# Recurrence products on the full 128x128 array with one readout burst per pair, a pinned first solve, and LoRA grouped with the first block as 336 and 384 columns

## The chip, the core and the metric

The kernel runs on one core of one Trainium2 chip. A core has five engines that run side by side, each from its own queue in order: TensorE (PE) multiplies, with a weight loader beside it (PEld); VectorE (DVE), ScalarE (ACT) and GpSimd (POOL) do elementwise work; SyncE (SP) issues most of the DMA transfers. They wait for one another through semaphores. TensorE takes two operands from the on-chip memory SBUF, a stationary one and a moving one of up to 512 columns here, and writes to PSUM.

The metric is the device time in microseconds (us), the median of three runs. Before the change it is 1944.83 us (1944.59 to 1945.52).

## The reference, cut to what matters

All arrays are float32; 256 frames (tokens), model width 4096. One layer is computed:

```python
proj = x @ w_in                       # 256 x 4096 by 4096 x 16592
fq, fk, fv, ff, r, k, v, wd, ad, z = split(proj)   # 2048 each; ff 16; wd, ad 96; z 4096
# first head group: forgetting attention, 16 heads of 128
log_f = log_sigmoid(ff + f_bias);  c = cumsum(log_f)
fox = softmax(fq.fk/sqrt(128) + c[t] - c[s], s <= t) @ fv
# second head group: RWKV-7, 32 heads of 64, after a two-tap token shift of r, k, v, wd, ad
decay = exp(-exp(-softplus(-(w0 + tanh(wd) @ w_up)) - 0.5));  a = sigmoid(a0 + ad @ a_up)
kk = normalise(k * k_k);  k = k * (1 + (a - 1) * k_a)
for t in frames:                      # state S is 64 x 64 for each head
    S = S * decay[t] + (S @ -kk[t]) (kk[t] * a[t])^T + v[t] k[t]^T
    y[t] = S @ r[t]
rwkv = groupnorm(y) * gain + bias + sum(r * k * r_k) * v
h = concat(fox, rwkv) * silu(z)
out = layernorm(2 ** 0.25 * x + h @ w_out)
```

By work this is two large products, 256 x 4096 by 4096 x 16592 and 256 x 4096 by 4096 x 4096, with attention and a recurrence of 256 steps between them.

## The kernel before, in words

**The weight products.** Every fp32 operand of a large product is cut in two fp32r numbers, hi and lo, by `split`: ACT copies the high part (L137), DVE subtracts it (L138). `mm` then makes three products for each weight tile, x_hi by w_hi, x_lo by w_hi and x_hi by w_lo (L143, L144, L145), each with a 128x128 stationary slice of x and 512 moving columns of weights. Tiles `w_5h` and `w_5l` are the parts of one weight load, and `acc` is the PSUM sum.

**The LoRA stage (L107 to L166)** comes first, while x itself arrives, in 17 pieces of one or two k-tiles. Each piece loads x, the 208 columns of wd, ad and ff (`w_lora`) and 512 columns of the first weight block, splits them, and multiplies the 208 columns into `accl0`, `accl1` and the 512 into `acc0_0_0`, `acc0_0_1`.

**The blocks.** The rest of w_in is a stream of 8 x 4 blocks: for each of eight head pairs n, block 0 holds r and k, block 1 the two v, blocks 2 and 3 attention's q and k and the gate. A block has 16 loads of 1024 columns by 128 rows (two k-tiles; SP issues them at L213), 12 products each. The load buffers form a ring of four, the hi parts of four, the lo parts of three. A name such as w0_3_7l is pair 0, block 3, load 7, low part.

**The side work.** All else runs in the gaps of the block loop: after every second (k-tile, half) step, `slot()` moves each of a list of generators one `yield` on. `ahead()` runs `lora()` and then `prepare(i)` for the 16 slices of two heads; `chain()` runs `forget()` (the forget gate, which ends with the DMA `ncd`, L346) and then `rwkv(n)` for the eight pairs; `unload` and `fox` carry q, k and the gate to the attention. `yield from wait(k)` lets k slots go by. So the slot counts set where a side product stands among the weight products. A scheduler then orders each engine's queue from the program and its own model of durations; where `tc.keep_in_program_order` is put round an instruction, it stays behind its predecessor in the program.

**`rwkv(n)` (L510 to L704)** works on one pair n: two slices u of 128 rows, each with two heads j of 64, and four chunks c of 64 frames. In order:

- `gp`: score products of each chunk, masked into `gb` and `Nb`.
- the solve (L582 to L590): 31 steps, each a DVE multiply into `prod` (L584) and a reduction into `xc` (L587), which invert the triangular matrices inside the chunks. A step works on one column more than the step before it, and `next(other)` lets the transposes of `turns()` go between. Only the first step is kept in program order. For n = 0 the attention scores `lg` (L723) and the splits of the next weights share that queue.
- the result `td` is stored and reloaded in another layout (T, X): X is the inverse, block-diagonal over the two heads.
- the chunk loop (L652 to L684): `residual(c)` makes `rh` = lt . SV (L631), copied by DVE to R; `up` = X . R (L658), copied by ACT to UV; `sp` = BKt . UV (L667), from which DVE makes the next chunk's state in SV; and `yp`, the readout (L683), eight products for each slice and chunk pair, 64 by 64 by 64.

In `rh`, `sp` and `yp` each head j has its own tile, `lt[j]`, `SV[j]`, `UV[j]`, and is zero outside its part. An operand `lt0_n` has the rows of both heads; j picks the 64 columns in which the result is wanted:

```python
nc.tensor.matmul(rh[HALF[j], u * C : (u + 1) * C], lt[j][:, u, c, 0:C], SV[j][:, u, c, :], start=True, stop=True)
```

So a product uses 128 rows and 64 stationary columns, and two of them lie side by side in the array. `up` uses a 128x128 stationary operand with 64 moving columns.

After the eight pairs the output product takes 8 x 16 loads of w_out, then the residual, LayerNorm and the store follow.

Of the kernel before, what the change touches and what calls it, by code (L numbers as in the profile page):

```python
# [10 lines left out]
F32 = mybir.dt.float32  # L11
# [49 lines left out]
QS = 2 * S // B  # L61

# [20 lines left out]
def layer(ctx: ExitStack, tc: tile.TileContext, xt, xtok, w_lora, w_main, muv, w_o, up, par, mulora, fbias, lng, lnb, cst, out):  # L83
# [27 lines left out]
    for n, (k0, k1) in enumerate(pieces):  # L111
# [3 lines left out]
        raw = spool.tile([P, 2 * LW], F32, tag="lr", name=f"lr{n}", bufs=4)  # L115
        (nc.scalar if n < 3 else nc.sync).dma_start(out=raw[:, : (k1 - k0) * LW], in_=w_lora[:, k0:k1, :].rearrange("p k c -> p (k c)"))
        l_raw.append(raw)
        raw = wpool.tile([P, 1024], F32, tag="wr", name=f"wr{n}", bufs=4)
        nc.sync.dma_start(out=raw[:, : (k1 - k0) * OB], in_=w_main[0, 0][:, k0:k1, :].rearrange("p k c -> p (k c)"))
# [34 lines left out]
    for n, (k0, k1) in enumerate(pieces):  # L154
# [303 lines left out]

    def prepare(i):
# [7 lines left out]
        if u == 0:  # L467
# [3 lines left out]
                lt=[rp.tile([P, 2, NCH, P], F32, tag=f"lt{j}", name=f"lt{j}_{n}") for j in range(2)],  # L471
# [12 lines left out]
        lt = [q["lt"][j][:, u] for j in range(2)]  # L484
        nc.scalar.copy(q["lc"][:, u, :], eL[:, :, C])
        nc.vector.scalar_tensor_tensor(lt[0][:, :, 0:C], ch(kr), nkk[:, i : i + 1], eL[:, :, 0:C], ALU.mult, ALU.mult)
        nc.vector.tensor_tensor(lt[0][:, :, C:P], ch(r), eL[:, :, 1:], ALU.mult)
# [22 lines left out]
    def rwkv(n):  # L510
# [4 lines left out]
        lc, BK, lt, bon = q["lc"], q["BK"], q["lt"], q["bon"]  # L515
        yield from wait(W["gp"])
        gp = [[pst(f"gp{n}_{u}_{j}") for j in range(2)] for u in range(2)]
        for u in range(2):
            for c in range(NCH):
                for j in range(2):  # L520
                    h = HALF[j]
                    nc.tensor.matmul(gp[u][j][:, c * P : (c + 1) * P], BK[h, u, c, :], lt[j][h, u, c, :], start=True, stop=True)  # L522
# [21 lines left out]
        for u in range(2):  # L544
            for j in range(2):
                o = HALF[1 - j]
                nc.vector.tensor_tensor(lt[j][o, u], gv[u][j][o], m(o), ALU.mult)
        SV = [rp.tile([P, 2, NCH, C], F32, tag=f"SV{j}", name=f"SV{j}_{n}") for j in range(2)]
# [537 lines left out]
```

## Time and profile before

| | |
|---|---|
| median of three runs | 1944.83 us (1944.59, 1944.83, 1945.52) |
| the profiled execution | 1945.32 us |
| its span (first to last instruction) | 1943.5 us |
| mean granted TensorE clock | 0.998 |
| PE busy | 1925.2 us, 99% |
| DVE, ACT, POOL busy | 1348.8, 962.8, 129.9 us |
| DMA traffic | 420.07 MB, 216 GB/s |
| LoRA stage on PE | from 4.24 to 70.8 us |

In the page and in the answers of the trace, busy times and starts are in us of the span's clock. A row of the timeline gives the start, the duration of one instruction in the pipeline, engine, line, operation, output tile <- input tiles, their sizes, and a count where like neighbours are put together. Matmuls overlap: what one costs is the distance from its start to that of the next, not its duration. An fp32 product (not fp32r) runs as two passes, so a product of the source counts twice there. A bracket at the end of a row says how long the engine was idle ahead of it, and what it was waiting for. The granted clock (PEclk) is the share of full speed that TensorE was given.

### The profile page before, as it was taken

How to read it: one execution, taken by the hardware profiler on the slowest of the kernel's cores; microseconds unless marked ns; L12 is line 12 of the kernel's file. 1: busy time of each engine (PE TensorE's matmuls, PEld its weight loads, DVE VectorE, ACT ScalarE, POOL GpSimd, SP SyncE). 2: the span in 40 equal slices, each digit the busy share in tenths (PEclk: the TensorE clock that was granted, in tenths of full speed). 3: DMA queues.
4: the chain of work that ended last, by engine and by line, in shares of the span. 5: the costliest groups of instructions: out<-in, count | busy, mean ns of one | idle time of the engine just before them, and what ended most of it. 6: DMA issues, size and time to landing. Idle time of an engine off the chain costs nothing.

```text
span 1943.5 us, 28242 instructions
## 1 busy us (share of the span) xinstructions
PE 1925.2 (99%) x10121; PEld 1578.9 (81%) x10121; DVE 1348.8 (69%) x2291; ACT 962.8 (50%) x1445; POOL 129.9 (7%) x207
## 2 busy tenths in 40 slices
PE   9998999999999999999999999999999999999998
PEld 8877788878887888788878887888788878888886
DVE  6577667866786678667856785778577856755555
ACT  6453465455545554465456445644564454433332
POOL 0020002000200020002000200020001000000000
PEclk9999999999999999999999999999999999999999
DMA  9577677867786768677867686778677878766664
GB/s 339 138 242 199 202 195 214 229 199 206 222 229 192 227 201 240 189 221 209 238 185 228 207 239 183 228 208 240 178 232 219 241 273 263 236 198 199 188 205 163
DMA packets 269393, 420.07 MB, mean 216 GB/s; under 512 B 142338, under 2 KB 171028, under 8 KB 269252
## 3 DMA queue, kind: packets, MB, share of 16 engines
q1 hardware_dynamic: 268820, 417.84, 72.3%
q8 instruction: 79, 1.29, 0.3%
q10 hardware_dynamic: 432, 0.43, 0.1%
q14 instruction: 62, 0.51, 0.1%
HBM read 388.55 MB, written 29.64 MB: 215 GB/s over the span
## 4 chain that ended last, share of the span: by engine, by line
PE 96%; DVE 2%; DMA 0%; issue 0%; ACT 0%; SPq 0%; ACTq 0%; DVEq 0%
PE acc L143 24%; PE acc L145 23%; PE acc L144 23%; PE oacc L853 6%; PE oacc L855 6%; PE oacc L854 6%; PE yp L683 1%; PE gp L522 1%; PE up L658 1%; PE rh L631 1%; PE sp L667 0%; DVE prod L584 0%; DVE xc L587 0%; PE tp L555 0%; PE fsp L718 0%
## 5 line engine op out<-in xcount | busy, mean ns | idle before, releaser
L587 DVE TENSOR_REDUCE xc<-prod 128x8 f32<-128x16 f32 (+30 forms) x248 | 73.1, 295 | 6.7
L584 DVE TENSOR_TENSOR prod<-Nb,xc 128x8 f32<-128x8 f32 (+30 forms) x248 | 71.4, 288 | 6.6
L138 DVE TENSOR_TENSOR w_6l<-w,w_6h 128x1024 fp32r<-128x1024 f32 x31 | 37.9, 1223 | 45.3 <-ACT w_6h L137 29.1
L714 POOL TENSOR_SCALAR_AFFINE_SELECT nb<-nb 128x128 f32<-128x128 f32 x32 | 14.5, 455 | 727.5 <-DMA nb<-ncd 284.0
L138 DVE TENSOR_TENSOR w_5l<-w,w_5h 128x1024 fp32r<-128x1024 f32 x31 | 40.5, 1308 | 32.3 <-PE acc L145 31.3
L138 DVE TENSOR_TENSOR w_8l<-w,w_8h 128x1024 fp32r<-128x1024 f32 x31 | 37.8, 1218 | 30.2 <-ACT UV L661 13.6
L137 ACT CAST w_7h<-w 128x1024 fp32r<-128x1024 f32 x31 | 32.5, 1049 | 52.1 <-DMA w<-in_w_main_dram 34.3
L138 DVE TENSOR_TENSOR w_12l<-w,w_12h 128x1024 fp32r<-128x1024 f32 x31 | 37.9, 1223 | 26.7 <-issue 12.4
L145 PE MATMUL acc<-w_7l,x 128*128 128x512 f32 x124 | 48.7, 402 | 5.4 <-DVE w_7l L138 5.4
L137 ACT CAST w_13h<-w 128x1024 fp32r<-128x1024 f32 x31 | 32.6, 1051 | 40.7 <-DMA w<-in_w_main_dram 15.3
L138 DVE TENSOR_TENSOR w_7l<-w,w_7h 128x1024 fp32r<-128x1024 f32 x31 | 37.8, 1220 | 21.5 <-ACT sl L679 8.5
L143 PE MATMUL acc<-w_7h,x 128*128 128x512 f32 x124 | 51.3, 413 | 0.0
L137 ACT CAST w_5h<-w 128x1024 fp32r<-128x1024 f32 x31 | 32.6, 1052 | 37.5 <-PE acc L144 37.5
L138 DVE TENSOR_TENSOR w_14l<-w,w_14h 128x1024 fp32r<-128x1024 f32 x31 | 37.9, 1221 | 19.0 <-issue 16.2
L137 ACT CAST w_15h<-w 128x1024 fp32r<-128x1024 f32 x31 | 32.7, 1054 | 36.9 <-PE acc L144 27.2
L143 PE MATMUL acc<-w_5h,x 128*128 128x512 f32 x124 | 50.5, 407 | 0.0
L143 PE MATMUL acc<-w_3h,x 128*128 128x512 f32 x124 | 50.2, 405 | 0.0
L138 DVE TENSOR_TENSOR w_11l<-w,w_11h 128x1024 fp32r<-128x1024 f32 x31 | 37.9, 1222 | 17.6 <-PE acc L145 16.2
L143 PE MATMUL acc<-w_8h,x 128*128 128x512 f32 x124 | 50.1, 404 | 0.1
L143 PE MATMUL acc<-w_6h,x 128*128 128x512 f32 x124 | 49.9, 402 | 0.0
L137 ACT CAST w_10h<-w 128x1024 fp32r<-128x1024 f32 x31 | 32.5, 1049 | 35.0 <-PE acc L144 30.9
L143 PE MATMUL acc<-w_2h,x 128*128 128x512 f32 x124 | 49.6, 400 | 0.0
(810 smaller groups left out, 6520.0 us busy)
## 6 DMA issues: line engine op xcount, KB each, us to landing
w<-in_w_main_dram SPq DMA_DIRECT2D x496, 512.0 KB
wo<-in_w_o_dram SPq DMA_DIRECT2D x128, 512.0 KB
bt<-bk SPq DMA_DIRECT2D x88, 128.0 KB
Nb<-nd SPq DMA_DIRECT2D x16, 512.0 KB
wr<-in_w_main_dram SPq DMA_DIRECT2D x15, 512.0 KB
hd<-hl SPq DMA_DIRECT2D x29, 256.0 KB
h<-hd SPq DMA_DIRECT2D x29, 256.0 KB
raw<-bt SPq DMA_DIRECT2D x16, 256.0 KB
```

The lines of the kernel that those rows point to most:

```text
L137: nc.scalar.copy(hi[:, :n], src[:, :n])
L138: nc.vector.tensor_tensor(lo[:, :n], src[:, :n], hi[:, :n].bitcast(F32), ALU.subtract)
L143: nc.tensor.matmul(acc[:, :n], xs[k][:, 0, tt], hi[:, o : o + n], start=(k == 0), stop=False)
L144: nc.tensor.matmul(acc[:, :n], xs[k][:, 1, tt], hi[:, o : o + n], start=False, stop=False)
L145: nc.tensor.matmul(acc[:, :n], xs[k][:, 0, tt], lo[:, o : o + n], start=False, stop=(k == KT - 1))
L522: nc.tensor.matmul(gp[u][j][:, c * P : (c + 1) * P], BK[h, u, c, :], lt[j][h, u, c, :], start=True, stop=True)
L584: first = nc.vector.tensor_tensor(prod[:, :, :, s + 1 :], nb[:, :, s : s + 1, s + 1 :].to_broadcast([P, 2, NJ, w]), xc[:, :, :, s + 1 :], ...
L587: nc.vector.tensor_reduce(xc[:, :, :, s : s + 1], prod[:, :, :, s:], AX.X, ALU.add)
L631: nc.tensor.matmul(rh[HALF[j], u * C : (u + 1) * C], lt[j][:, u, c, 0:C], SV[j][:, u, c, :], start=True, stop=True)
L853: nc.tensor.matmul(acc, ht[k][:, 0, tt], hi, start=(k == 0), stop=False)
L854: nc.tensor.matmul(acc, ht[k][:, 1, tt], hi, start=False, stop=False)
L855: nc.tensor.matmul(acc, ht[k][:, 0, tt], lo, start=False, stop=(k == KT - 1))
```

## The change

Four things are changed.

- **Full products.** `lt[0]` and `lt[1]`, `SV[0]` and `SV[1]`, and the two UV become one tile each (`LT`, `SVt`, `UVt`), with j as an inner index. `rh` and `sp` are now one product for each slice u, 128 rows by 128 stationary columns by 128 moving columns, where four products of 64 by 64 stood for a pair of slices. Only the two blocks on the diagonal are wanted, which `diagonal` picks; the other two quarters of the result are not read. R and UV are now copied one half by ACT and one half by DVE; before, DVE copied R whole and ACT both halves of UV.
- **One readout burst.** `yp` leaves the chunk loop. Its 32 products of the four chunks come in one piece behind the last `up`, and a `wait(2)` after `sp` takes the slots.
- **First solve.** For n = 0 every step's multiply stands in program order, for the other pairs the first alone, as before.
- **Columns.** The first 128 columns of the first block move to the LoRA products: 336 and 384 columns for 208 and 512. The sums are copied to `bk0_0` from both, and `lw` takes another buffer (that of `vs`).

```diff
@@ the LoRA stage
-        hi, lo = split(l_raw[n], (k1 - k0) * LW, f"wl{n}", spool, str(n % 3), 2 * LW)
+        hi, lo = split(l_raw[n], (k1 - k0) * LA, f"wl{n}", spool, str(n % 3), 2 * LA)
         for j, m in steps(k1 - k0, False):
-            mm(acc_l[m], m, k0 + j, hi, lo, j * LW, LW)
-        hi, lo = split(w_raw[n], (k1 - k0) * OB, f"wr{n}")
+            mm(acc_l[m], m, k0 + j, hi, lo, j * LA, LA)
+        hi, lo = split(w_raw[n], (k1 - k0) * LB, f"wr{n}")
         for j, m in steps(k1 - k0, k1 == KT):
-            mm(acc_0[m], m, k0 + j, hi, lo, j * OB, OB)
+            mm(acc_0[m], m, k0 + j, hi, lo, j * LB, LB)
...
-    lw = rp.tile([P, 2, LW], F32, tag="bk", name="lw")
+    lw = rp.tile([P, 2, LW], F32, tag="vs", name="lw", bufs=1)
+    bk_0 = rp.tile([P, 2, OB], F32, tag="bk", name="bk0_0")
     for m in range(2):
         nc.scalar.copy(lw[:, m, :], acc_l[m][:, :LW])
+        nc.scalar.copy(bk_0[:, m, :P], acc_l[m][:, LW:LA])
...
+    def left(t, j):
+        return t.rearrange("p u c (x j t) -> p u c j x t", x=2, j=2)[:, :, :, j]
...
@@ rwkv(n)
-        SV = [rp.tile([P, 2, NCH, C], F32, tag=f"SV{j}", name=f"SV{j}_{n}") for j in range(2)]
-        UV = [rp.tile([P, 2, NCH, C], F32, tag=f"UV{j}", name=f"UV{j}_{n}") for j in range(2)]
+        SVt = rp.tile([P, 2, NCH, 2, C], F32, tag="SV", name=f"SV{n}")
+        UVt = rp.tile([P, 2, NCH, 2, C], F32, tag="UV", name=f"UV{n}")
+        SV = [SVt[:, :, :, j, :] for j in range(2)]
+        UV = [UVt[:, :, :, j, :] for j in range(2)]
...
             first = nc.vector.tensor_tensor(prod[:, :, :, s + 1 :], nb[:, :, s : s + 1, s + 1 :].to_broadcast([P, 2, NJ, w]), xc[:, :, :, s + 1 :], ALU.mult)
-            if not t:
+            if not t or not n:
                 tc.keep_in_program_order(first)
...
             for u in range(2):
-                for j in (1, 0):
-                    nc.tensor.matmul(rh[HALF[j], u * C : (u + 1) * C], lt[j][:, u, c, 0:C], SV[j][:, u, c, :], start=True, stop=True)
+                nc.tensor.matmul(rh[:, u * P : (u + 1) * P], LT[:, u, c, 0:P], flat(SVt[:, u, c]), start=True, stop=True)
             R = rp.tile([P, 2, C], F32, tag="R", name=f"R{n}_{c}", bufs=2)
-            nc.vector.tensor_copy(flat(R), rh[:, : 2 * C])
+            for j in range(2):
+                (nc.scalar.copy if j else nc.vector.tensor_copy)(R[HALF[j]], diagonal(rh, j))
             return R
+
+        def diagonal(t, j):
+            return t[HALF[j], : 2 * P].rearrange("p (u j t) -> p u j t", u=2, j=2)[:, :, j]
...
             for j in range(2):
-                nc.scalar.copy(UV[j][HALF[j], :, c, :], uv[HALF[j]])
+                (nc.vector.tensor_copy if j else nc.scalar.copy)(UV[j][HALF[j], :, c, :], uv[HALF[j]])
             yield
...
+            if c == NCH - 1:
+                break
+            sp = pst(f"sp{n}_{c}")
+            for u in range(2):
+                nc.tensor.matmul(sp[:, u * P : (u + 1) * P], BKt[:, u, c, :], flat(UVt[:, u, c]), start=True, stop=True)
...
+            yield from wait(2)
+        yp = pst(f"yp{n}")
+        for c in range(NCH):
             for u in range(2):
-                for lhs, rhs in ((SV, lt), (UV, gb)):
+                for V in (0, 1):
                     for j in (1, 0):
-                        nc.tensor.matmul(yp[HALF[j], u * S + c * C : u * S + (c + 1) * C], lhs[j][:, u, c, :], rhs[j][:, u, c, C:P], start=lhs is SV, stop=lhs is UV)
-            yield
+                        o = yp[HALF[j], u * S + c * C : u * S + (c + 1) * C]
+                        if V:
+                            nc.tensor.matmul(o, UV[j][:, u, c, :], gb[j][:, u, c, C:P], start=False, stop=True)
+                        else:
+                            nc.tensor.matmul(o, SV[j][:, u, c, :], lt[j][:, u, c, 1], start=True, stop=False)
+        yield
```

What the scheduler makes of it is shown at three places. The first is DVE's queue in the last block of pair 0, where the first solve stands (prod and xc are its two instructions of a step, with the width growing to 31; the splits are w0_3_...l, the attention scores lg0). Before:

```order
L584 TENSOR_TENSOR prod0_1697<-Nb0_1553,xc0_1698 128x8x29
L587 TENSOR_REDUCE xc0_1698<-prod0_1697 128x8
L584 TENSOR_TENSOR prod0_1697<-Nb0_1553,xc0_1698 128x8x30
...
L584 TENSOR_TENSOR prod0_1697<-Nb0_1553,xc0_1698 128x8x31
...
L138 TENSOR_TENSOR w0_3_7l_1867<-w0_3_7_1810,w0_3_7h_1866 128x1024
L723 SCALAR_TENSOR_TENSOR lg0_1968<-fsp0_1965,ct_845,nb0_1909 128x128
L723 SCALAR_TENSOR_TENSOR lg0_1968<-fsp0_1965,ct_845,nb0_1909 128x256
L138 TENSOR_TENSOR w0_3_8l_1892<-w0_3_8_1840,w0_3_8h_1891 128x1024
```

All 31 steps stand ahead of w0_3_7l there. After (the line numbers are those of the changed kernel: L595 and L598 are the solve's two, L140 the split, L742 the scores):

```order
L140 TENSOR_TENSOR w0_3_6l_1842<-w0_3_6_1779,w0_3_6h_1841 128x1024
L595 TENSOR_TENSOR prod0_1696<-Nb0_1554,xc0_1697 128x8x12
L598 TENSOR_REDUCE xc0_1697<-prod0_1696 128x8
L595 TENSOR_TENSOR prod0_1696<-Nb0_1554,xc0_1697 128x8x13
...
L140 TENSOR_TENSOR w0_3_7l_1866<-w0_3_7_1809,w0_3_7h_1865 128x1024
L595 TENSOR_TENSOR prod0_1696<-Nb0_1554,xc0_1697 128x8x14
...
L595 TENSOR_TENSOR prod0_1696<-Nb0_1554,xc0_1697 128x8x15
...
L742 SCALAR_TENSOR_TENSOR lg0_1967<-fsp0_1964,ct_848,nb0_1908 128x128
L742 SCALAR_TENSOR_TENSOR lg0_1967<-fsp0_1964,ct_848,nb0_1908 128x256
L140 TENSOR_TENSOR w0_3_8l_1891<-w0_3_8_1839,w0_3_8h_1890 128x1024
```

Two steps now stand between successive splits, so steps 16 to 31 have moved behind w0_3_8l; the order of the scores and w0_3_8l stays.

The second is PE's queue in pair 1, the residual of chunk 1 (rh, then up) among the weight products of pair 2's first block. Before:

```order
L145 MATMUL acc2_0_1_3983<-w2_0_3l_4029,x6_323 128x512
L631 MATMUL rh1_1_4126<-SV1_1_3303,lt1_1_2884 64x64
L631 MATMUL rh1_1_4126<-SV0_1_3302,lt0_1_2883 64x64
...
L143 MATMUL acc2_0_0_3982<-w2_0_3h_4028,x7_326 128x512
L144 MATMUL acc2_0_0_3982<-w2_0_3h_4028,x7_326 128x512
```

The two rh rows come twice, once for each slice. After:

```order
L147 MATMUL acc2_0_1_3969<-w2_0_3l_4015,x7_326 128x512
L641 MATMUL rh1_1_4106<-SV1_3290,lt1_2872 128x128 x2
L145 MATMUL acc2_0_0_3968<-w2_0_4h_4057,x8_361 128x512
L146 MATMUL acc2_0_0_3968<-w2_0_4h_4057,x8_361 128x512
L147 MATMUL acc2_0_0_3968<-w2_0_4l_4058,x8_361 128x512
L145 MATMUL acc2_0_1_3969<-w2_0_4h_4057,x8_361 128x512
L146 MATMUL acc2_0_1_3969<-w2_0_4h_4057,x8_361 128x512
L147 MATMUL acc2_0_1_3969<-w2_0_4l_4058,x8_361 128x512
L145 MATMUL acc2_0_0_3968<-w2_0_4h_4057,x9_364 128x512
L671 MATMUL up1_1_4124<-R1_1_4109,X_834 128x64 x2
```

Four products of 64 by 64 became two of 128 by 128, and up stands seven weight products behind them.

The third is SP's queue right after the LoRA stage (w0_1_... are weight loads, muv0 the shift coefficients of v, bt0_0 the store of the first block for its turn, ncd the forget gate). Before:

```order
L894 DMA muv0_860<-in_muv_dram 128x256
L213 DMA w0_1_7_1015<-in_w_main_dram 128x1024
L276 DMA bt0_0_1000<-bk0_0_857 64x16x32 x3
L346 DMA ncd_844<-flg_943 16x256
L276 DMA bt0_0_1000<-bk0_0_857 64x16x32
L213 DMA w0_1_8_1035<-in_w_main_dram 128x1024
```

After:

```order
L915 DMA muv0_862<-in_muv_dram 128x256
L278 DMA bt0_0_1002<-bk0_0_842 64x16x32 x4
L350 DMA ncd_847<-flg_945 16x256
L215 DMA w0_1_7_1017<-in_w_main_dram 128x1024
L278 DMA raw0_1035<-bt0_0_1002 128x2x256
L215 DMA w0_1_8_1037<-in_w_main_dram 128x1024
```

The load w0_1_7 has moved from ahead of ncd to behind it, and raw0 has come ahead of w0_1_8.

More of the change, by code (lines that the diff above doesn't have):

```diff
@@ L514, in rwkv @@
         q = pairs[n]
-        lc, BK, lt, bon = q["lc"], q["BK"], q["lt"], q["bon"]
+        lc, BK, LT, bon = q["lc"], q["BK"], q["lt"], q["bon"]
+        lt = [left(LT, j) for j in range(2)]
         yield from wait(W["gp"])
@@ L885, in layer @@
                 slot()
[L886 removed]
+            bk = rp.tile([P, 2, OB], F32, tag="bk", name=f"bk{n}_{b}") if n or b else bk_0
             for m in range(2):
@@ L889, in layer @@
                     nc.scalar.copy(bk[:, m, : 2 * P], acc[m][:, : 2 * P])
+                elif not n and not b:
+                    nc.scalar.copy(bk[:, m, P:], acc[m][:, :LB])
                 else:
```

58 lines of the change are left out of this document (28 added, 30 removed).

## The prediction

> **What bounds the kernel now.** I read the page's busy table first, then who TensorE (PE) waited for, then the timeline of the places that the edits touch.
>
> ```profile
> span 1943.5 us, 28242 instructions
> PE 1925.2 (99%) x10121; PEld 1578.9 (81%) x10121; DVE 1348.8 (69%) x2291; ACT 962.8 (50%) x1445; POOL 129.9 (7%) x207
> ```
>
> PE is busy all through, so only two things can save time: PE work made shorter, and PE waits removed. The waits of PE (engine, line, who it waited for: total, times, longest):
>
> ```profile
> PE acc L145 <- DVE w_7l L138: 5.4, 1, 5.4
> PE acc L145 <- DVE w_10l L138: 1.3, 1, 1.3
> ```
>
> The first is in the first pair's solve. Its PE timeline (start, duration, line, tiles), with the window's row behind it (after the five engines' busy times, PEclk is the granted clock):
>
> ```profile
> 186.07 0.39 PE L144 MATMUL acc<-w_7h,x 128*128 128x512 f32 x1
> 191.82 0.79 PE L145 MATMUL acc<-w_7l,x 128*128 128x512 f32 x1 [5.36 <-DVE w_7l L138]
> ...
> 197.85 0.40 PE L144 MATMUL acc<-w_8h,x 128*128 128x512 f32 x1
> 199.28 0.73 PE L145 MATMUL acc<-w_8l,x 128*128 128x512 f32 x2 [1.04 <-DVE w_8l L138]
> ...
> 224.70 0.39 PE L145 MATMUL acc<-w_1l,x 128*128 128x512 f32 x1
> ```
> ```profile
> 192.00:198.00 6.00, 6.00 (x18) 4.69 (x18) 0.65 (x2) 0.00 (x0) 0.00 (x0) 0.60 0.32 87
> ```
>
> What its products cost at full clock is read from two other places of PE's timeline, the LoRA stage (twelve products of 208 columns, then twelve of 512) and a later attention burst:
>
> ```profile
> 42.31 0.26 PE L143 MATMUL accl<-wl10h,x 128*128 128x208 f32 x1
> ...
> 43.64 0.41 PE L143 MATMUL acc<-wr10h,x 128*128 128x512 f32 x1
> ```
> ```profile
> 46.39 0.26 PE L143 MATMUL accl<-wl11h,x 128*128 128x208 f32 x1
> ```
> ```profile
> 391.28 0.39 PE L145 MATMUL acc<-w_8l,x 128*128 128x512 f32 x1
> 391.51 0.38 PE L717 MATMUL fsp<-fk,fq 128*128 128x128 f32 x2
> 391.73 0.60 PE L718 MATMUL fsp<-fk,fq 128*128 128x256 f32 x2
> ...
> 392.39 0.40 PE L144 MATMUL acc<-w_8h,x 128*128 128x512 f32 x1
> ```
>
> Twelve products in 43.64 to 46.39 are 0.229 us each; the burst, from the last weight product ahead of it to the second one behind it less two regular steps, is 1.11 - 0.46 = 0.65. From 186.07 to 197.85 PE starts 14 weight products and one such attention burst, 3.9 us at full clock. It took 11.8, so 7.9 us are lost: a wait, and then a granted clock of 0.60.
>
> **Part 1: the solve pinned for the first pair.** The loss arises because 25 solve instructions stand ahead of w_7l on DVE. In the new order two solve steps stand between successive splits, so w_7l comes after 13 steps, in time: gain 7.9. But what stood ahead of w_7l now lies behind w_8l, where DVE has less room. DVE's rows there:
>
> ```profile
> 177.13 0.29 DVE L584 TENSOR_TENSOR prod<-Nb,xc 128x128 f32<-128x128 f32 x1
> ...
> 190.55 1.22 DVE L138 TENSOR_TENSOR w_7l<-w,w_7h 128x1024 fp32r<-128x1024 f32 x1
> ```
> ```profile
> 198.01 1.22 DVE L138 TENSOR_TENSOR w_8l<-w,w_8h 128x1024 fp32r<-128x1024 f32 x1
> ...
> 205.34 1.22 DVE L138 TENSOR_TENSOR w_12l<-w,w_12h 128x1024 fp32r<-128x1024 f32 x1
> ...
> 213.26 0.42 DVE L371 SCALAR_TENSOR_TENSOR h<-fo,zf 128x256 f32<-128x256 f32 x1 [1.81 <-ACT fo L740]
> ...
> 216.34 1.23 DVE L138 TENSOR_TENSOR w_0l<-w,w_0h 128x1024 fp32r<-128x1024 f32 x1 [0.63 <-issue]
> ...
> 220.25 1.23 DVE L138 TENSOR_TENSOR w_1l<-w,w_1h 128x1024 fp32r<-128x1024 f32 x1
> ```
>
> Between w_8l's start and the end of the next block's w_1l the new DVE order holds: the work of 198.01 to 205.34 (7.3, without a gap), four splits w_12l to w_15l (4 x 1.14, a split's 1.22 less what it overlaps with its successor), h and its remainder (0.7), w_0l with the value means and SV (216.34 to 220.25: 3.9), w_1l (1.2), and now solve steps 16 to 31: 177.13 to 190.55 less one split, 12.3. Sum 30.0 us. PE gives it from 198.01 to 224.70 = 26.7. So DVE ends some 3.3 us late and PE waits that long in small pieces, at w_9l, w_10l and w_1l. The wait at w_8l stays: the attention scores still stand ahead of it. Net **-4.6 us**. Ends: -7.9 (interleaved independent instructions overlap and close the gap) and -2. The solved T's store and reload move by three weight loads on SP's queue; they are read only after the next block's w_6l, five weight groups (some 13 us) past w_1l, which covers them. If that cover were gone the four X transposes would wait, and the recurrence behind them, not the weight products.
>
> **Part 2: full products in the recurrence.** I price a burst as the attention burst above, since entry and exit cost time too.
>
> ```profile
> 241.06 0.39 PE L145 MATMUL acc<-w_6l,x 128*128 128x512 f32 x1
> 241.29 0.55 PE L658 MATMUL up<-R,X 128*128 128x64 f32 x4
> ...
> 241.97 0.39 PE L144 MATMUL acc<-w_6h,x 128*128 128x512 f32 x1
> ...
> 242.89 0.40 PE L145 MATMUL acc<-w_6l,x 128*128 128x512 f32 x1
> 243.22 0.46 PE L667 MATMUL sp<-UV,BKt 128*64 128x64 f32 x8
> ...
> 244.41 0.39 PE L144 MATMUL acc<-w_7h,x 128*128 128x512 f32 x1
> ...
> 245.34 0.40 PE L145 MATMUL acc<-w_7l,x 128*128 128x512 f32 x1
> 245.66 0.45 PE L631 MATMUL rh<-SV,lt 128*64 128x64 f32 x8
> ...
> 246.38 0.40 PE L144 MATMUL acc<-w_7h,x 128*128 128x512 f32 x1
> ```
> ```profile
> 261.65 0.40 PE L145 MATMUL acc<-w_11l,x 128*128 128x512 f32 x1
> 261.98 0.34 PE L683 MATMUL yp<-lt,SV 128*64 128x64 f32 x4
> ...
> 262.93 0.40 PE L144 MATMUL acc<-w_11h,x 128*128 128x512 f32 x1
> ```
>
> An fp32 product shows as two passes (x4 is two products). Costs: up 0.91 - 0.46 = 0.45 for 4 full-array passes; rh 1.04 - 0.46 = 0.58 for 8 passes on half the columns; sp with yp (24 half passes) 1.52 - 0.46 = 1.06; yp alone (16) 1.28 - 0.46 = 0.82. So a half pass costs (1.06 - 0.82)/8 = 0.03 and a half-column burst some 0.34 more than its passes; a full pass costs 0.11 (fsp: two passes of 128 columns in 0.22), and a full burst next to nothing more (4 x 0.11 = 0.44 against 0.45).
>
> The new rh and sp are 4 full passes with 128 moving columns. The nearest rows are up (same stationary size, 64 columns) and fsp (128 columns): they give 0.45 and 0.44. Per pair, before: rh in its first place, right behind xp, 0.38 (from its first start to the next weight product); three rh 1.74; three sp with yp 3.18; one yp 0.82: 6.12. After: first rh 0.44; three rh 1.35; three sp 1.35; one yp burst of 64 passes 0.82 + 48 x 0.03 = 2.26: 5.40. up is unchanged. Saved 0.72 a pair, times eight: **-5.8 us**. Ends: -6.2 (0.44 a burst, all yp overhead shared) and +0.6 (a full burst as dear as rh now, 0.58).
>
> Moved with it: R and UV are now copied half by ACT, half by DVE, so a product waits for the later of two queues. In the new order up stands seven weight products behind rh (six in the first chunk), sp five or six behind up, and on DVE the UV copy stands right behind R and ahead of the next split; what is queued behind it are splits with two weight groups in hand. I price this at nothing; a split (1.22) in front of a copy would use up the cover, 5 x 0.229 = 1.15 plus the burst's own 0.45. The extra slot per chunk makes a pair end about three slots later; nothing on PE waits for that, since the next prepare begins a block later.
>
> TensorE Tiling (Array Packing), section Overview, in the Trainium skill promises up to 2x for dimensions of 64 or less, against this change. The passes here agree (eight packed in 0.24, four full in 0.44); by that alone the recurrence would lose, which the second rival prices. The same page, section Tiling Modes, says that a change of tiling mode drains the array: the 0.34 is what that looks like here, and the sum above goes by the row.
>
> **Part 3: 336 and 384 columns.** Beside the 208 and 512 columns of the LoRA rows above, six products of 256:
>
> ```profile
> 281.47 0.28 PE L421 MATMUL lp<-lr,uph 96*128 96x256 f32 x1
> ...
> 282.18 0.40 PE L143 MATMUL acc<-w_2h,x 128*128 128x512 f32 x1
> ```
>
> 208 columns take 1.33/12 = 0.111 us (42.31 to 43.64), 512 take 0.229, 256 take 0.71/6 = 0.118: below 256 columns the time no longer falls. One pair of products costs 0.340 now. After, on the line through 256 and 512 columns, 0.153 + 0.173 = 0.326; in proportion to 512, 0.322. That is 14 to 18 ns on 192 pairs, 2.7 to 3.5 us. The first group's split is larger by 128 columns (0.15 us on DVE by the split's 1.22 for 1024, as much on ACT), before PE can start: -0.3. I take **-2.5 us**; ends -3.5 and 0 (if 256 were already on a floor that rises to 512 evenly from 208).
>
> TensorE: Matmul & The Clock Gate, Back-to-back issue gap, in the Trainium skill gives a product N/2.4 + 2.5 ns; by that the new pair would take 0.305 and the part would save an estimated 3 to 6 us, but the 512 row (0.229 against its 0.216) stands above it.
>
> **Part 4: what follows the LoRA stage.** SP's queue there:
>
> ```profile
> 88.84 0.33 SPq L346 DMA_DIRECT2D ncd<-flg  x1
> ...
> 90.43 0.60 SPq L213 DMA_DIRECT2D w<-in_w_main_dram  x1
> ```
>
> ncd waits for the forget gate and holds back the weight loads behind it. Before, w_8 was the first of these; in the new order w_7 is, one group (12 x 0.229 = 2.7 us) earlier for PE. On the other side the gate now ends ahead of w_7l's split on DVE, and the splits w_8l to w_10l are spread among the prepare work, which should end the 1.3 us wait at w_10l. Ends -1.3 and +2.7; nearest to nothing, **0**.
>
> **The sum.** -4.6 - 5.8 - 2.5 + 0 = -12.9. The profiled execution took 1945.3 us, 0.5 above the median of 1944.8, and its span is 1943.5, so 1.8 lies around it and stays. 1945.3 - 12.9 = **1932.4 us**, 0.66% faster.
>
> **Rivals.** (a) DVE cannot carry the solve among the splits: the 3.3 us late become the whole 7.9, because each split of the next block starts late too. For it: 30.0 against 26.7 us. Against it: behind w_1l DVE has a split of 1.2 per group of 2.7 us and recovers. 1937.
>
> (b) Packed products were the cheaper form: a full burst keeps the 0.34 of entry and exit on top of 0.44, so rh and sp cost 0.78. Six such bursts give +2.0 a pair against the 5.40: 7.4 for 6.1 before, +10 us in all, 1945.3 - 7.1 + 10 = 1948. For it: the eight against four passes. Against it: up has the same form and costs 0.45. It undoes the other gains from 0.72 us a burst on.
>
> (c) The split copies come late: each of 56 up and sp bursts waits for the slower queue. At 0.3 us each this is +17 and the kernel is slower, 1949; it decides above 0.23. For it: 1.22 us splits on both queues' way. Against it: the order, and a cover of 1.6 us.
>
> (d) The solve's gain comes whole (7.9) and w_10l's wait goes: 1928.
>
> **How the numbers follow.** Forecast as summed 0.60, (a) 0.13, (d) 0.12, (b) 0.05, (c) 0.03, anything else on the slow side 0.07. The range 1926.5 to 1939.5 takes in the forecast's ends, (a) and (d), 0.85 in all. A change of 0.2% (3.9 us) is about what a measurement of this kernel can tell. Faster: forecast, (a), (d) and 0.03 of the rest, 0.88; same, the other 0.04 of the rest; slower, (b) and (c), 0.08.
>
> **What would show it.** Right: no PE wait for w_7l, granted clock 1.00 there, small waits at w_9l, w_10l and w_1l of about 3 us; rh, sp and up bursts of equal cost near 0.45, one yp burst near 2.3; 336 and 384 columns spaced 0.15 and 0.17. Wrong: rh or sp at 0.6 or more; waits of up or sp for R or UV; a wait for w_7h behind ncd.

## The result, and the profile after

The changed kernel takes 1937.16 us, the median of five runs (1936.05 to 1939.13), against 1944.83 before: ratio 0.9960, 95% interval 0.9946 to 0.9975, that is 4.9 to 10.5 us faster. The profiled execution is the shortest of the five, 1936.05 us, 9.3 below the profiled one of before. The forecast was 1932.4 in a range of 1926.5 to 1939.5. The sign and the range held. The sum did not: 12.9 us were forecast and some 8 came. The solve gave more than its share of them, and the recurrence, the largest term, next to nothing.

The page's first rows and the waits of PE in the changed kernel:

```profile
span 1934.3 us, 27820 instructions
PE 1920.1 (99%) x9897; PEld 1592.7 (82%) x9897; DVE 1362.9 (70%) x2323; ACT 964.2 (50%) x1447; POOL 123.6 (6%) x207
```
```profile
PE acc L147 <- DVE w_1l L140: 1.1, 1, 1.1
PE acc L147 <- DVE w_8l L140: 1.0, 1, 1.0
PE xp L656 <- DVE Q L636: 1.0, 1, 1.0
...
PE acc L147 <- DVE w_10l L140: 0.2, 1, 0.2
```

The wait for w_7l (5.4) is gone, w_10l's has gone from 1.3 to 0.2, w_8l's stands at 1.0 as before, and two of about 1 us are new: w_1l in the block behind the first solve, and xp in the last pair.

Both kernels make the same weight products, so the start of the same product in both PE timelines tells where the time went. A second profile of the changed kernel (span 1935.2), taken with the last experiments, stands beside the first:

| start of | before | after | difference | second profile | its difference |
|---|---|---|---|---|---|
| first weight product | 4.24 | 4.39 | +0.15 | 4.42 | +0.18 |
| block 1 of pair 0 (end of the LoRA stage) | 70.83 | 69.45 | -1.38 | 69.43 | -1.40 |
| block 2 of pair 0 | 120.13 | 117.22 | -2.91 | 118.62 | -1.51 |
| block 3 of pair 0 (the first solve) | 166.81 | 163.88 | -2.93 | 165.28 | -1.53 |
| block 0 of pair 1 | 221.53 | 210.96 | -10.57 | 212.38 | -9.15 |
| block 1 of pair 1 (behind the first recurrence) | 275.67 | 266.08 | -9.59 | 267.31 | -8.36 |
| block 1 of pair 7 (behind six more recurrences) | 1429.25 | 1419.17 | -10.08 | 1419.91 | -9.34 |
| first product of w_out | 1568.18 | 1558.15 | -10.03 | 1558.90 | -9.28 |
| 192 products on (behind the last recurrence) | 1623.41 | 1614.43 | -8.98 | 1615.38 | -8.03 |
| last weight product | 1930.25 | 1921.00 | -9.25 | 1921.93 | -8.32 |

So the LoRA stage gave some 1.4, the block behind it 1.5 in one profile and 0.1 in the other, and the block with the first solve 7.6. The next block, with the wait for w_1l and the first recurrence, gave 0.8 to 1.0 back. Six middle recurrences together gave 0.5 to 1.0, where the forecast had 0.72 each, and the last one cost 1.0 to 1.3.

**The first solve.** The place of the old stall on PE with its window (the number behind the five busy times is the granted clock), and then DVE's rows there:

```profile
186.99 0.40 PE L146 MATMUL acc<-w_8h,x 128*128 128x512 f32 x1
188.43 0.74 PE L147 MATMUL acc<-w_8l,x 128*128 128x512 f32 x2 [1.04 <-DVE w_8l L140]
```
```profile
186.00:192.00 6.00, 4.80 (x21) 3.30 (x20) 5.50 (x14) 2.75 (x6) 0.00 (x0) 1.00 0.28 87
```
```profile
180.33 0.29 DVE L598 TENSOR_REDUCE xc<-prod 128x8 f32<-128x128 f32 x1
186.50 0.74 DVE L742 SCALAR_TENSOR_TENSOR lg<-fsp,ct,nb 128x128 f32<-128x128 f32 x2 [5.88 <-PE fsp L737]
187.16 1.22 DVE L140 TENSOR_TENSOR w_8l<-w,w_8h 128x1024 fp32r<-128x1024 f32 x1
```

No stall at w_7l, and the clock stays at 1.00. What is left at w_8l is not the solve's: DVE has finished step 15 at 180.6 and stands idle for 5.88 us, because the attention scores are next in its order and PE's score product comes only at 185.6. About eight of the sixteen steps that are left would have fitted into that time, by an estimate from the old kernel's rows, where a step of this width takes 0.66 to 0.76 us. All sixteen follow behind w_8l, and w_1l comes late; whether the idle time is the reason is tried below.

**A chunk of the recurrence.** The first pair's second chunk, PE with DVE and ACT:

```profile
237.04 0.39 PE L147 MATMUL acc<-w_7l,x 128*128 128x512 f32 x1
...
237.27 0.61 PE L641 MATMUL rh<-SV,lt 128*128 128x128 f32 x4
...
237.52 1.23 DVE L140 TENSOR_TENSOR w_10l<-w,w_10h 128x1024 fp32r<-128x1024 f32 x1 [1.39 <-ACT sl L691]
...
237.94 0.39 PE L146 MATMUL acc<-w_8h,x 128*128 128x512 f32 x1
```
```profile
238.78 0.28 DVE L644 COPY R<-rh 64x128 f32<-64x128 f32 x1
...
239.10 0.26 ACT L644 COPY R<-rh 64x128 f32<-64x128 f32 x1 [0.76 <-DVE R L644]
239.10 0.40 PE L145 MATMUL acc<-w_8h,x 128*128 128x512 f32 x1
239.41 0.52 PEld L671 LDWEIGHTS up<-R,X 128*128 128x128 f32 x4 [0.35 <-ACT R L644]
239.41 0.66 PE L671 MATMUL up<-R,X 128*128 128x64 f32 x4
...
240.19 0.40 PE L147 MATMUL acc<-w_8l,x 128*128 128x512 f32 x1
```

The rh burst costs 237.94 - 237.04 - 0.46 = 0.44, against 0.58 before. But up costs 240.19 - 239.10 - 0.46 = 0.63, against 0.45. Its two halves of R come one behind the other. DVE's half stands behind the split of w_10l, which is released just as the burst begins: it starts 0.48 us after the start of the last product that reads w_7l, whose buffer it takes. 231 of this kernel's splits ahead of which DVE was idle start at just this distance, so that product releases w_10l, and not ACT's sl, which the bracket names. ACT's half of R then waits for DVE's (the bracket), though it reads other partitions of rh. R is ready at 239.36, 0.26 after the start of the last weight product ahead of up. The wait shown on PE is short: the regular start would have been 239.33. But before, the weight loader took X while the last weight product ran, whose row at 241.06 stands in the prediction:

```profile
241.06 0.64 PEld L658 LDWEIGHTS up<-R,X 128*128 128x128 f32 x4
```

Now the load, too, waits for R and lies open.

**The readout burst and the LoRA stage.**

```profile
254.76 0.39 PE L147 MATMUL acc<-w_12l,x 128*128 128x512 f32 x1
255.08 0.34 PE L702 MATMUL yp<-lt,SV 128*64 128x64 f32 x4
...
257.43 0.39 PE L146 MATMUL acc<-w_13h,x 128*128 128x512 f32 x1
```
```profile
41.92 0.31 PE L145 MATMUL accl<-wl10h,x 128*128 128x336 f32 x1
```
```profile
43.75 0.33 PE L145 MATMUL acc<-wr10h,x 128*128 128x384 f32 x1
...
45.85 0.31 PE L145 MATMUL accl<-wl11h,x 128*128 128x336 f32 x1
```

The burst of 64 passes costs 2.67 - 0.46 = 2.21 (forecast 2.26). Twelve products of 336 columns take 1.83, twelve of 384 take 2.10: 0.153 and 0.175, a pair 0.328 for 0.340.

### The profile page after: what moved, and what is told of

It reads as the page before. It is cut to its first block, busy times and chain, and to the rows that moved or that the text cites. A ratio compares the mean times of both kernels' runs of the same rounds, so it can differ in the third digit from the quotient of the medians.

```text
span 1934.3 us, 27820 instructions
## 1 busy us (share of the span) xinstructions
PE 1920.1 (99%) x9897; PEld 1592.7 (82%) x9897; DVE 1362.9 (70%) x2323; ACT 964.2 (50%) x1447; POOL 123.6 (6%) x207
## 4 chain that ended last, share of the span: by engine, by line
PE 95%; DVE 2%; DMA 2%; ACT 0%; issue 0%; SPq 0%; DVEq 0%; ACTq 0%
PE acc L145 23%; PE acc L147 23%; PE acc L146 23%; PE oacc L872 6%; PE oacc L874 6%; PE oacc L873 6%; PE up L671 1%; PE gp L531 1%; PE rh L641 1%; PE sp L680 1%; DMA Nb<-nd 0%; PE accl L147 0%; PE accl L146 0%; PE accl L145 0%; PE yp L702 0%; PE yp L700 0%
## 5 line engine op out<-in xcount | busy, mean ns | idle before, releaser
L598 DVE TENSOR_REDUCE xc<-prod 128x8 f32<-128x16 f32 (+30 forms) x248 | 73.1, 295 | 6.5
L595 DVE TENSOR_TENSOR prod<-Nb,xc 128x8 f32<-128x8 f32 (+30 forms) x248 | 71.4, 288 | 6.5 <-DMA Nb<-nd 0.2
L140 DVE TENSOR_TENSOR w_6l<-w,w_6h 128x1024 fp32r<-128x1024 f32 x31 | 37.9, 1221 | 43.1 <-ACT w_6h L139 29.2
L140 DVE TENSOR_TENSOR w_5l<-w,w_5h 128x1024 fp32r<-128x1024 f32 x31 | 41.3, 1333 | 28.2 <-PE acc L147 25.8
L140 DVE TENSOR_TENSOR w_12l<-w,w_12h 128x1024 fp32r<-128x1024 f32 x31 | 37.9, 1223 | 27.7 <-issue 14.4
L140 DVE TENSOR_TENSOR w_10l<-w,w_10h 128x1024 fp32r<-128x1024 f32 x31 | 37.9, 1222 | 24.3 <-issue 19.7
L140 DVE TENSOR_TENSOR w_8l<-w,w_8h 128x1024 fp32r<-128x1024 f32 x31 | 37.8, 1219 | 20.2 <-PE acc L147 10.5
L140 DVE TENSOR_TENSOR w_0l<-w,w_0h 128x1024 fp32r<-128x1024 f32 x31 | 37.9, 1223 | 19.1 <-PE acc L147 17.8
L140 DVE TENSOR_TENSOR w_7l<-w,w_7h 128x1024 fp32r<-128x1024 f32 x31 | 37.9, 1221 | 19.0 <-PE acc L147 13.1
L139 ACT CAST w_12h<-w 128x1024 fp32r<-128x1024 f32 x31 | 32.5, 1048 | 37.4 <-DMA w<-in_w_main_dram 21.9
L140 DVE TENSOR_TENSOR w_4l<-w,w_4h 128x1024 fp32r<-128x1024 f32 x31 | 37.8, 1219 | 18.8 <-issue 11.8
L140 DVE TENSOR_TENSOR w_11l<-w,w_11h 128x1024 fp32r<-128x1024 f32 x31 | 37.8, 1220 | 18.1 <-PE acc L147 18.1
L140 DVE TENSOR_TENSOR w_1l<-w,w_1h 128x1024 fp32r<-128x1024 f32 x31 | 37.9, 1223 | 17.9 <-PE acc L147 17.6
L145 PE MATMUL acc<-w_15h,x 128*128 128x512 f32 x124 | 49.6, 400 | 0.0
L147 PE MATMUL acc<-w_1l,x 128*128 128x512 f32 x124 | 48.5, 391 | 1.1 <-DVE w_1l L140 1.1
```

What stands on the lines that cost most here:

```text
L139: nc.scalar.copy(hi[:, :n], src[:, :n])
L140: nc.vector.tensor_tensor(lo[:, :n], src[:, :n], hi[:, :n].bitcast(F32), ALU.subtract)
L145: nc.tensor.matmul(acc[:, :n], xs[k][:, 0, tt], hi[:, o : o + n], start=(k == 0), stop=False)
L147: nc.tensor.matmul(acc[:, :n], xs[k][:, 0, tt], lo[:, o : o + n], start=False, stop=(k == KT - 1))
L595: first = nc.vector.tensor_tensor(prod[:, :, :, s + 1 :], nb[:, :, s : s + 1, s + 1 :].to_broadcast([P, 2, NJ, w]), xc[:, :, :, s + 1 :], ...
L598: nc.vector.tensor_reduce(xc[:, :, :, s : s + 1], prod[:, :, :, s:], AX.X, ALU.add)
```

## The experiments

### The three parts alone

The recurrence part alone: the diff without the lines on LoRA and without this one.

```diff
-            if not t or not n:
+            if not t:
```

> Only the recurrence part of the change: full products, one readout burst a pair, the copies of R and UV divided between ACT and DVE; first solve and LoRA columns as before. Theory (the cheaper products are real, but up now waits for R): rh 0.45, sp 0.45, yp burst 2.22, up 0.51 to 0.69 instead of 0.456; a middle pair gains 0.1 to 0.2 us, the last pair loses about 1, so the whole lies within 1 us of before. The forecast's own sum: up stays at 0.456, 0.72 a pair is saved, 5.8 us faster than before.

1945.42 us (median of ten) against 1945.88 of before on the same chip: ratio 1.0002, 0.9992 to 1.0011. The theory holds: the part by itself gives nothing. In this trace a middle pair gains 0.2, 2.3 us are gained up to the first product of w_out, and the last recurrence loses 2.65. There xp waits 1.1 us for its operand from DVE, and the granted clock falls behind it:

```profile
1572.00:1577.00 5.00, 4.83 (x49) 4.21 (x49) 2.48 (x5) 2.56 (x6) 0.00 (x0) 0.68 1.04 394
```

The same row shows the DMA engines full (share 1.04, 394 GB/s): in the last block the reloads of h and the weight loads share them, in every kernel here.

The pin alone:

```diff
-            if not t:
+            if not t or not n:
```

> Only the pinned first solve. Theory: the 7.6 us of the block with the solve are gained whole (no wait for w_7l, granted clock 1.00), and about 1.3 come back as a wait for w_1l in the next block, so 6.4 us faster than before. The forecast's sum: 4.6 faster. Rival: the 1.5 us that the block after the LoRA stage gained belong to this part as well, then 7.9 faster.

1938.45 us, ratio 0.9967 (0.9954 to 0.9980), 7.4 us at the medians. In the trace the block with the solve gains 7.6, the next one gives 1.1 back, 6.9 at the end. Its waits of PE:

```profile
PE acc L145 <- DVE w_10l L138: 1.2, 1, 1.2
PE acc L145 <- DVE w_8l L138: 1.0, 1, 1.0
PE acc L145 <- DVE w_1l L138: 0.8, 1, 0.8
```

In the trace the theory's size holds. The interval of the times (3.9 to 9.0 us) would also take in the forecast's 4.6 and the rival's 7.9; but the block behind the LoRA stage gains only 0.3 here and its wait for w_10l is still there, so the going of that wait is not this part's.

The columns alone: before, with the lines of the diff on `LA`, `LB`, `lw` and `bk_0`.

```diff
-LW = 2 * LORA + NF
+LW = 2 * LORA + NF
+LA = LW + P
+LB = OB - P
```

> Only the 336 and 384 columns. Theory: a pair of products goes from 0.340 to 0.328 us, the first three pieces lose 0.6, so the LoRA stage ends 1.4 us earlier; and the block behind it gains 1.5 since the order of DVE and SP there comes from this part: 2.9 us faster than before. Rival: that 1.5 belongs to another part, 1.4 faster. The forecast's sum: 2.5 in the stage and nothing behind it.

1942.69 us (median of ten), ratio 0.9985 (0.9976 to 0.9995), 3.2 us at the medians. The LoRA stage ends 2.1 us earlier in this trace and the next block gains 1.05, since its w_10l is no longer waited for. That is near the theory's 2.9. But the second profile of the whole change gained only 0.1 in that block: there, PE waits for w_8h instead.

```profile
95.86 0.50 PE L145 MATMUL acc<-w_8h,x 128*128 128x512 f32 x1 [1.11 <-ACT w_8h L139]
```

So this gain differs between executions by more than 1 us.

### Who makes up late

Both halves of R copied by ACT:

```diff
-                (nc.scalar.copy if j else nc.vector.tensor_copy)(R[HALF[j]], diagonal(rh, j))
+                nc.scalar.copy(R[HALF[j]], diagonal(rh, j))
```

> The changed kernel with both halves of R copied by ACT, nothing on DVE. Theory A (R is late because its DVE half stands behind a split that is released just ahead of it): R is ready about 0.4 us earlier, up goes back to 0.456, 0.6 us a pair, 4 to 5 us faster than the changed kernel, span near 1930. Rival B (the hand-over from DVE to ACT alone is the loss): also faster, by the same. Rival C (up costs more because its place is in the middle of a tile's three products): up stands six products behind rh again, so also faster; B and C are told apart by a kernel in which DVE copies both halves. If up stays at 0.63, all three fall.

1933.19 us (median of four, 1932.64 to 1937.52), ratio 0.9943 (0.9928 to 0.9957). The profiled execution was the slowest of these (ACT waited 8.1 us for the load of w_15 in the full DMA stretch, 5.1 in the changed kernel), so the chunk is shown from the repeat below; in both, up costs 0.45 at the median of 32, and sp, rh and yp are as in the changed kernel. All three theories predicted this; the next kernel divides the first two. Both halves by DVE:

```diff
-                (nc.scalar.copy if j else nc.vector.tensor_copy)(R[HALF[j]], diagonal(rh, j))
+                nc.vector.tensor_copy(R[HALF[j]], diagonal(rh, j))
```

> The changed kernel with both halves of R copied by DVE. Theory A (R is late because it stands behind a split on DVE): two copies of 0.28 behind the same split are as late as one on DVE and one on ACT; up stays at 0.6 to 0.7, time as the changed kernel. Rival B (the hand-over from DVE to ACT is the loss): up falls to 0.46, 4 to 5 us faster than the changed kernel.

```profile
238.76 1.23 DVE L140 TENSOR_TENSOR w_10l<-w,w_10h 128x1024 fp32r<-128x1024 f32 x1 [1.37 <-ACT sl L691]
...
240.02 0.59 DVE L644 COPY R<-rh 64x128 f32<-64x128 f32 x2
...
240.34 0.40 PE L145 MATMUL acc<-w_8h,x 128*128 128x512 f32 x1
...
240.75 0.63 PE L671 MATMUL up<-R,X 128*128 128x64 f32 x4
...
241.51 0.39 PE L147 MATMUL acc<-w_8l,x 128*128 128x512 f32 x1
```

1943.15 us in its one run. There is no hand-over between engines any more, yet up costs 0.71, and a middle pair takes 0.27 us more than in the changed kernel. So the hand-over is not the cause (B falls).

Theory A is only half of it, too: the old kernel shows a split ahead of R that costs nothing. In the third chunk of every middle pair a split stood right ahead of R's copy on DVE there, as in this one of the first pair:

```profile
252.08 1.23 DVE L138 TENSOR_TENSOR w_11l<-w,w_11h 128x1024 fp32r<-128x1024 f32 x1 [1.41 <-ACT sl L679]
...
253.34 0.29 DVE L633 COPY R<-rh 128x128 f32<-128x128 f32 x1
253.56 0.40 PE L145 MATMUL acc<-w_9l,x 128*128 128x512 f32 x1
253.80 0.55 PE L658 MATMUL up<-R,X 128*128 128x64 f32 x4
...
254.47 0.40 PE L144 MATMUL acc<-w_9h,x 128*128 128x512 f32 x1
```

Up costs 254.47 - 253.56 - 0.46 = 0.45. R was copied whole in 0.29 and was ready at 253.63, 0.07 after the start of the last weight product. A split and one whole copy are in time; a split and two halves in a row, 0.58 to 0.59 in all, are late, on one engine or on two. So it takes both. No run puts a whole copy behind the split in the changed kernel; by the rows above the first half alone was ready at 239.06, ahead of the 239.10 at which that product starts.

Rival C, the place of up in the middle of a tile's three products, can carry little: in the packed kernel below up stands at the same place and costs 0.51 (mean of 32).

### Packing and grouping by themselves

rh and sp taken back to half-column products (sp likewise, with the copies' views to match):

```diff
-                nc.tensor.matmul(rh[:, u * P : (u + 1) * P], LT[:, u, c, 0:P], flat(SVt[:, u, c]), start=True, stop=True)
+                for j in (1, 0):
+                    nc.tensor.matmul(rh[HALF[j], u * C : (u + 1) * C], lt[j][:, u, c, 0], SV[j][:, u, c, :], start=True, stop=True)
```

> The changed kernel with rh and sp taken back to four half-column products for each slice pair, all else (slots, one readout burst, copies divided) as changed. Theory (a half-column burst costs 0.34 beyond its passes, a full one nothing): rh 0.59, sp 0.56 to 0.59, the first rh 0.06 cheaper; 0.7 us a pair, 5 to 6 us slower than the changed kernel. Rival (the full form saves only together with the burst, being no cheaper by itself): rh and sp stay near 0.45 and the time is the same. By TensorE Tiling (Array Packing), Overview, in the Trainium skill the packed form would be up to twice as fast.

1940.97 us in its one run, just above the ten of the changed kernel (1936.05 to 1940.93), so the rows must decide. The rh row and its neighbours:

```profile
238.65 0.39 PE L147 MATMUL acc<-w_7l,x 128*128 128x512 f32 x1
...
238.97 0.45 PE L642 MATMUL rh<-SV,lt 128*64 128x64 f32 x8
...
239.68 0.39 PE L146 MATMUL acc<-w_8h,x 128*128 128x512 f32 x1
```

rh 0.57 here (0.58 at the median), sp 0.59, the first rh 0.06 cheaper: the theory's prices. A middle pair is only 0.4 us longer, not 0.7, since up now waits less for R (0.51 for 0.59, means of 32): 0.3 of the 0.7 that the cheaper rh and sp give is lost in that wait. The rival, that the full form saves nothing alone, falls. TensorEngine Tiling (Array Packing), Overview, in the Trainium skill promises up to twice the speed for the packed form. Here, between weight products, it was the dearer one by 0.13 us a burst.

The readout taken back into the loop, a burst of 16 behind each sp and one at the end:

```diff
+            read(c)
             yield from wait(2)
-        yp = pst(f"yp{n}")
-        for c in range(NCH):
```

> The changed kernel with the readout yp taken back into the chunk loop, behind sp, all else as changed. Theory (each readout burst pays its entry again, the passes are the same): sp with yp 0.45 + 0.82 = 1.27 in place of 0.45, the last yp 0.82 in place of 2.22; 3 x 0.82 - 1.40 = 1.06 us a pair, 8.5 us slower than the changed kernel. Rival (full and half-column products next to each other drain once more): more than that, sp with yp 1.4 or above. Rival (entry is shared by the burst as in before): sp with yp near 1.06, about 2 us slower.

```profile
608.79 0.39 PE L147 MATMUL acc<-w_2l,x 128*128 128x512 f32 x1
609.02 0.61 PE L693 MATMUL sp<-UV,BKt 128*128 128x128 f32 x4
609.55 0.34 PE L675 MATMUL yp<-lt,SV 128*64 128x64 f32 x4
...
610.50 0.39 PE L146 MATMUL acc<-w_3h,x 128*128 128x512 f32 x1
```

sp with yp costs 1.71 - 0.46 = 1.25 (theory 1.27), the bursts of a middle pair add up to 1.02 us more (theory 1.06; the pair itself is 1.3 us longer in the trace), and the whole takes 1946.06 us in its one run. Against before (1.06) full sp products beside a half-column readout are a loss: for sp the full form pays only because the readout left the loop.

### Versions that go further

The first pair's solve at two steps in three slots, on top of R on ACT:

```diff
+            if not n and t % 2:
+                yield
```

> The kernel with R on ACT, and the first pair's solve spread over half as many slots again (two steps in three slots instead of two in two). If the waits for w_8l (1.0 us), w_9l (0.2) and w_1l (0.7 to 1.1) come from solve steps that DVE cannot carry among the splits, they shrink: w_1l's goes, about 1 to 2 us gained up to the end of the next block. Rival: w_8l waits for the attention scores ahead of it, not for the solve, and stays at 1.0.

1947.23 us in its one run. The waits for w_9l and w_1l went, as the theory said, and w_8l's stayed at 1.0, as the rival said. But the later solve moved every later piece of side work by slots, with waits for w_7l (three, 6.4 us in all) and others: some 13 us are lost against R on ACT by the end of the third pair.

The last four kernels ran side by side on one chip, five times each. The changed kernel again, and R on ACT again:

> The changed kernel once more, as the partner of the next three on one chip: median 1936 to 1938, as in its first runs.

> R on ACT once more, next to the changed kernel on one chip. By the traces a middle pair is 0.73 us shorter: 3 to 5 us faster than the changed kernel, ratio to the kernel before near 0.994.

1938.15 us, ratio to before 0.9964 (0.9951 to 0.9976), and 1933.77, ratio 0.9942 (0.9929 to 0.9954). The chunk with R on ACT:

```profile
237.62 0.61 PE L641 MATMUL rh<-SV,lt 128*128 128x128 f32 x4
237.64 1.05 ACT L139 CAST w_11h<-w 128x1024 fp32r<-128x1024 f32 x1 [0.24 <-ACT sl L691]
...
238.59 0.53 ACT L644 COPY R<-rh 64x128 f32<-64x128 f32 x2
...
239.22 0.40 PE L147 MATMUL acc<-w_8l,x 128*128 128x512 f32 x1
239.46 0.55 PE L671 MATMUL up<-R,X 128*128 128x64 f32 x4
...
240.13 0.39 PE L146 MATMUL acc<-w_8h,x 128*128 128x512 f32 x1
```

Here, too, R stands behind a piece of work for the splits, ACT's cast of w_11h, and its halves run in a row, 0.53 in all. But the cast begins 0.24 ahead of DVE's split (237.64 against 237.88) and takes 1.05 for 1.23. R is ready at 239.12, before the last weight product ahead of up has begun, and up costs 0.45. A middle pair is 0.83 us shorter than before the change, and the last weight product starts at 1916.83, 13.4 before that of the old kernel.

The first head's attention scores kept in program order on DVE, and then also the reloads of h started earlier:

```diff
+            if not i:
+                tc.keep_in_program_order(s)
```
```diff
-BACK = 10
+BACK = 6
```

> R on ACT, and the first head's attention scores kept in program order on DVE, which puts them behind the split w_8l. Theory: w_8l's wait of 1.2 us is the scores' (DVE stands idle 5.9 us ahead of them, waiting for PE's score products), and the 1.3 us wait for w_1l follows from that idle time; both go, 1.5 to 2.5 us faster than R on ACT alone at the end of the next block. Rival: the scores are now late for the products behind them (fpt), and PE waits there instead, no gain.

> As the one before, with the reloads of h in the last block started four k-tiles earlier (BACK 6 for 10). Theory: from about 1550 us on the DMA engines are full (390 GB/s), w_15h waits 5 to 8 us for its load, and the last pair's xp burst costs 2.9 to 3.3 us instead of 1.6; an earlier start ends the full stretch before the last pair's products, 1 to 2 us faster. Rival: the rate is the same, one reload for each k-tile, so the weights only come late sooner: no change or slower.

1936.37 us, ratio 0.9954 (0.9941 to 0.9968), and 1934.89, ratio 0.9943 (0.9930 to 0.9955). With the scores moved, DVE goes on to w_8l at once, and PE's wait there is gone; but w_1l's grows:

```profile
180.36 0.29 DVE L598 TENSOR_REDUCE xc<-prod 128x8 f32<-128x128 f32 x1
181.17 1.23 DVE L140 TENSOR_TENSOR w_8l<-w,w_8h 128x1024 fp32r<-128x1024 f32 x1 [0.52 <-ACT w_8h L139]
```
```profile
PE acc L147 <- DVE w_1l L140: 1.4, 1, 1.4
```

The block with the solve gains 1.2 over R on ACT and the next one loses 2.4, by the scheduler's new order. So the first half of the theory holds (the wait was the scores') and the second falls (w_1l does not follow from it). The earlier reloads gave 2.0 us at the last recurrence in the trace; in the times the difference of these two kernels lies within their intervals. Neither beats R on ACT alone, which beats both kernels of this case.

## Why the prediction was right or wrong, point by point

**The bound and the sign.** Right: PE stays 99% busy, and the change is faster because a PE stall goes.

**Part 1, the solve.** The mechanism was right, the size was not: -4.6 was forecast, with 3.3 us coming back in small waits. Measured alone, 7.6 went and 1.1 came back. The working put all of DVE's work between w_8l and w_1l end to end, 30.0 us against PE's 26.7; the trace has it in 28.2 (187.16 to 215.4), as a split or a step starts on DVE before an independent one ahead of it ends. The wait at w_8l stayed, as said, and for the reason given. (By the old kernel's trace 27 solve instructions, not 25, ran on DVE between w_6l and w_7l; nothing in the sum hangs on it.)

**Part 2, the recurrence.** The failed step is the one that reads "I price this at nothing", on the divided copies of R and UV. It said that the UV copy stands behind R and ahead of the next split, and that a split ahead of a copy would use up the cover. That happened at the other copy, R, in all but the first chunk of a middle pair: the change puts three of its four rh on a load's boundary, where PE's last use of a lo buffer releases a split; before, one stood there. But the split alone cost nothing in that one. What the step left out is that the two halves of R run one behind the other, 0.58 us in place of 0.29. Late waits of up for R stood in the prediction as a sign of being wrong. That is rival (c), with 0.18 to 0.24 us at three ups in four and 0.05 at the first, in place of the 0.3 at 56 places it named; sp did not pay. The prices of the bursts all held: full products 0.45, the readout burst 2.21 for 2.26, entry and exit gone. Up ate them: 4 x 0.45 became 0.50 + 0.63 + 0.63 + 0.69 in a middle pair, +0.64 of the 0.79 that the rest saved. With R on ACT a pair gains 0.83, for the 0.72 forecast. The whole trace is then 13.4 shorter, where 12.9 were forecast; that these two agree is luck, as other terms differ. Rival (b), packed cheaper, is refuted by the full bursts of the changed kernel at 0.44 and by the packed kernel.

**What was not in the sum.** The last recurrence lost 1.0 to 1.3: xp waits for an operand that DVE makes late while the DMA engines are full. Before, and with the solve or the columns alone, the DMA engines are as full and xp does not wait, so the wait comes with the recurrence part. With the earlier reloads it is gone. What sets DVE's lateness there was not tried beyond that.

**Part 3, the columns.** -2.5 was forecast, -1.4 to -1.5 came (-2.1 alone). A pair of products costs 0.328, by the line's 0.326: 2.3 us over 192 pairs. The start of the stage cost the rest, some 0.9 where 0.3 was charged; with the columns alone it cost 0.2 to 0.3, as charged. It differs between executions: the third piece's products begin 0.65 later than before in one profile of the changed kernel, 0.42 later in the other, and 0.26 earlier with the columns alone. In the eleven profiles with this stage it ends 0.6 to 2.1 us earlier than before. What sets this was not followed. By the formula of TensorE: Matmul & The Clock Gate, Back-to-back issue gap, in the Trainium skill, which the page gives for an isolated product, a pair would be 0.305; the trace has 0.328. The saving of 3 to 6 us that the prediction draws from it does not follow: the old pair has as many columns and would be 0.305 as well, where the trace had 0.340.

**Part 4.** 0 was taken, and a gain of 0.1 to 1.5 came. w_10l's wait went, as one end of the step said; in the second profile a wait of 1.1 for w_8h took its place. The other end, a wait of PE for w_7h behind ncd, came to 0.2 in the first profile.

**The errors met.** The solve gave about 2 more than forecast and the block behind the LoRA stage up to 1.5 more, the recurrence about 6 less and the columns 1 less. So the range held while the largest term was wrong, and that is luck: errors of opposite sign met.

## What to carry to other kernels

When a product's operand is copied out of PSUM between weight products, look in the order for what stands ahead of that copy on its engine at the moment of the burst, not only behind it, and add the copy's own length; a split released at the same product boundary is worth 1.2 us of lateness here, which a whole copy of 0.29 survived and two halves in a row did not. A copy divided over two engines is ready no sooner where the second half waits for the first, so give it to the engine whose queue is clear first. And price a burst between weight products by its kind of entry: take half-column products together in one burst, and make the rest full-array ones.

## What the runs showed of the hardware that was not expected

- A late operand costs more than its wait: in up, 0.08 us past the regular start cost 0.18 (0.63 for 0.45), since the weight load, hidden before, lay open. In the middle pairs of the old and the changed kernel up cost 0.45 where R was ready up to 0.07 us after the start of the weight product ahead of it, and 0.50, 0.63 and 0.69 where it was ready 0.13, 0.25 and 0.31 after.
- A half-column burst cost 0.57 to 0.59 with eight passes, a full one of twice the columns 0.45 with four, in pair after pair; a half-column burst right behind a full one added 0.81, what it costs by itself, so nothing was shared between the two kinds.
- A wait of 1.1 us in front of the last pair's products was followed by a granted clock of 0.68 over the next 5 us in the kernel with the recurrence part alone, and by 1.00 behind a wait of 1.0 us at the same place in the changed kernel.
